# The second table's rows of the first token tile, gathered by token and summed on TensorE in 32-column strips

## The chip, the cores and the metric

The kernel runs on one core of a Trainium2 chip. The metric is the device time of one execution in microseconds (us); lower is better. PE is TensorE, PEld its weight loads, DVE VectorE, ACT ScalarE, POOL GpSimd, SP SyncE. A line of the kernel is written L842.

## The reference

One decoder layer on 512 tokens of 1024 channels: a token mixer (dilated and differential attention, gated, projected), then a retrieval over 16,384 single-neuron experts. The retrieval is what the change touches:

```python
q = (xt @ w_q).reshape(t, 8, 2, 128)               # 8 heads, two half queries
sc = einsum('thpd,pkd->thpk', q, sub_keys)         # 128 keys for each half
top_s, top_i = top_k(sc, 16)                       # 16 best of each half
...                                                # 16 best pairs of the 256: ids, gates
u = u_tab[ids]                                     # first table's rows (1024 channels)
act = gelu(einsum('cd,chkd->chk', x, u))
vv = v_tab[ids]                                    # second table's rows
out = einsum('chk,chkd->cd', gates * act, vv)      # 8 x 16 = 128 rows summed for each token
```

Then follow a second residual and a last norm. All of it is float32.

## The kernel before

The tokens are worked in two halves of two tiles of 128 tokens each. For each half, `mixer(b)` does both attentions, and `tail(b)` the gates, projections, second norm and the scores of the retrieval with their best keys. Weights come as units of 512 KB through a ring of seven places (`shared`, `wraw`); a unit is split into a high and a low part (ACT L290; DVE or POOL L291), and `mm3` (L379) multiplies in three products.

The retrieval is done in two ways. Tiles 2 and 3 (the second half) go through all experts: a table of gates is built (the loop with L1162 to L1175, here the table stage), and then 64 pairs of experts go through `s_part` (L379 into `s_ps`) and `v_part` (L1154 into `acc`): the expert stage. Tiles 0 and 1 (the first half) go by rows: `gather` (L812) is an indirect DMA that brings, for slot s, one row of a table for each of the 128 tokens of a tile, 128 x 1024 numbers, 512 KB, into a place of the same ring of seven. A slot is one of the 128 chosen pairs of a token. A row of the first table (u) is multiplied by the token's input and summed over the channels on DVE (L842). A row of the second table (v) is scaled by the slot's activation of each token and added to a sum on DVE (L852), or on PE (L871): for the first 56 slots of tile 0 (`NPE`), `by_rows_pe` (L863) has ACT write a diagonal matrix of the activations (L868), and PE multiplies it with the row into `pe_acc` (two matmuls of 512 columns).

The rows are side work for the second half of the tokens and for the expert stage. `by_rows` (L829) is a generator that issues one row at each step: 128 slots of u for tile 0, then 128 of u for tile 1, then 72 of v for tile 0, then 128 of v for tile 1. `pump(k)` (L323) lets it go on by `RATE[k]` rows (L38) at each weight unit, attention block, or slot of the table: "w" 2 for each weight unit of `mixer(1)`, "a" 0.75 for each attention block, "b" 2, "o1" 1.5 and "q1" 1.25 for each unit in `tail(1)`, "G" 0.45 for each of 64 steps of the table, "c" 0.76 for each of 256 units of the expert stage. `pump("")` issues what is left at the end. `pump_pe` (L875) does the same for the rows on PE, "pt" 2 for each of 16 heads in `choose_late`, and "pG" 0.4 for each step of the table. `ahead` (L818) gathers one row ahead (`LOOK`).

PSUM has eight banks. Until `tail(1)` comes to its scores the pool `ps` has three banks for products (`mm`), two for transposes (`tp`), two for scores and one for outputs; there `late_psum` (L1027) closes it and opens one with two banks for the row sums and one `tp`.

The instructions are put in order on each engine when the program is built; each engine then runs its own in that order.

Of the kernel before, what the change touches and what calls it, by code (L numbers as in the profile page):

```python
# [11 lines left out]
F32 = mybir.dt.float32  # L12
# [10 lines left out]
P = 128  # L23
# [25 lines left out]
NPE = 56  # L49
# [36 lines left out]
def block(ctx, tc, x, cT, w_ada, bT, b_row, g1T, norm2_g, w_in, w_pa, w_pb, w_out, lq1, lk1, lq2, lk2,  # L86
# [24 lines left out]
    def place_of(kind, nm, dt=F32):  # L111
        """a unit among the weights' places: raw, high and low parts; a third of the parts only in the front"""
# [8 lines left out]
    def front_place(i):  # L121
        """sixteen units of the front, none of which waits for another's place"""
# [24 lines left out]
    def rsqrt(v, n, nm):  # L147
        """1/sqrt(v), [P, n]"""
# [23 lines left out]
    # ---- small operands  # L172
# [18 lines left out]
    # ---- silu(c)  # L191
# [5 lines left out]
    # ---- modulation: sums over the eight rows of a partition, then over the partitions  # L197
# [24 lines left out]
    def first_modulation(i):  # L222
        """shift and scale of the channels 256 i .. 256 i + 256"""
# [22 lines left out]
    def mod_rows(sec, t):  # L246
        """sections 2..5 of the modulation, a row each in DRAM; the second scale with its norm's weights"""
# [25 lines left out]
    # ---- first norm  # L273
# [80 lines left out]
    def cols(src, kt, c0, nm):  # L354
        """128 columns, for use as the stationary side"""
# [11 lines left out]
    def cols256(src, kt, c0, nm):  # L367
        """256 columns, for use as the moving side"""
# [4 lines left out]
    def mm3(out_ps, a, b, kt, last=0):  # L373
        """sum over k of a.T @ b, both in two parts; last: the side whose low part is used last"""
# [10 lines left out]
    # ---- relative position bias, as bands  # L385
# [20 lines left out]
    def bias_band(t, h, at, o, m, w):  # L406
        """t[p, at + i w + j] = vec[head, o + i LEN_D + p + j], i < m: rows of a block in reverse"""
# [4 lines left out]
    # ---- lambda  # L412
# [16 lines left out]
    # queries by head: head s of a pair keeps its half of the rows, the other half is zero. The queries of a block  # L429
    # stand in reverse, as the bands do; the transpose of the outputs turns them back.  # L430
# [12 lines left out]
    # ---- keys and values of the first half wait in DRAM for the second  # L443
# [3 lines left out]
    def query(hin, c0, q, nm):  # L447
        """q: [P, 2, HW]"""
# [8 lines left out]
    def key(b, hin, c0, k, i):  # L457
        """k: [P, T]"""
# [24 lines left out]
    # ---- dilated attention: the three groups of a head share one softmax, which is what their merge by  # L483
    # denominators amounts to
# [87 lines left out]
    def diff_finish(ob, dst, h0):  # L572
        """norm of two heads' outputs, ob: [P, 2, HW], transposed and split into dst"""
# [21 lines left out]
    def mixer(b, between):  # L595
        """attention of half b: both branches' outputs in two parts, channels on partitions"""
# [49 lines left out]
    # ---- the retrieval's choice  # L646
# [8 lines left out]
    def begin_topk(n, t):  # L655
        """t: [P, 768]"""
# [14 lines left out]
    # a pair of ranks (i, j) can be among the best sixteen only if (i + 1)(j + 1) <= 16: row 0 whole, eight of  # L671
    # rows 1..7, one of rows 8..15, in the order of the full table
# [4 lines left out]
    def choose(n, h0, nh, out):  # L677
        """row and column keys of the chosen pairs, heads h0 .. h0 + nh: two [P, 16 nh], a slot a column"""
# [150 lines left out]
    def by_rows(ids, gates, h2_row, make):  # L829
# [5 lines left out]
        for v, n, s in order:  # L835
# [5 lines left out]
            if v == 0:  # L841
                nc.vector.scalar_tensor_tensor(r, r, 1.0, h2, op0=ALU.mult, op1=ALU.mult, accum_out=a)  # L842
                if s == P - 1:
                    nc.scalar.activation(act[n], act[n], AF.Gelu_apprx_tanh)
                    nc.vector.tensor_mul(act[n], act[n], gates[n])
                    if n == 0:
                        on_pe.append(by_rows_pe(ids[0]))
# [383 lines left out]
```

## Time and profile before

| | |
|---|---|
| time, median of three runs | 2154.51 us (2152.59 to 2160.33) |
| span of the profiled execution | 2148.4 us |
| busy, share of the span | PE 87%, DVE 86%, POOL 59%, ACT 45% |
| DMA | 588.00 MB, mean 274 GB/s; gathers 268.47 MB of it |
| mean granted TensorE clock | 0.952 of full speed |

The page gives no separate time for the profiled execution: its span is 6.1 us under the median of the runs, and that difference stands for what lies around the span. A span is from the first instruction to the last. Busy time of an engine is the time in which one of its instructions ran.

### The profile page before, as it was taken

How to read it: one execution, taken by the hardware profiler on the slowest of the kernel's cores; microseconds unless marked ns; L12 is line 12 of the kernel's file. 1: busy time of each engine (PE TensorE's matmuls, PEld its weight loads, DVE VectorE, ACT ScalarE, POOL GpSimd, SP SyncE). 2: the span in 40 equal slices, each digit the busy share in tenths (PEclk: the TensorE clock that was granted, in tenths of full speed). 3: DMA queues.
4: the chain of work that ended last, by engine and by line, in shares of the span. 5: the costliest groups of instructions: out<-in, count | busy, mean ns of one | idle time of the engine just before them, and what ended most of it. 6: DMA issues, size and time to landing. Idle time of an engine off the chain costs nothing.

```text
span 2148.4 us, 34562 instructions
## 1 busy us (share of the span) xinstructions
PE 1875.4 (87%) x12324; PEld 1668.1 (78%) x12324; DVE 1839.9 (86%) x3515; ACT 970.7 (45%) x1725; POOL 1257.4 (59%) x797
## 2 busy tenths in 40 slices
PE   6999989887778799878687877889999999999995
PEld 6889889887666687768684455678988889998885
DVE  7757865689999999899889999978999898888777
ACT  2544575442333356543232366534444444444442
POOL 2323323456676676667675766667675665655564
PEclk9999999999999999989798999999999999999998
DMA  9968766758898999889956755788888999998886
GB/s 296 281 198 255 212 178 178 233 175 265 281 313 280 315 325 315 295 291 307 304 186 228 251 169 184 247 284 309 316 316 313 343 346 324 342 335 309 306 308 236
DMA packets 369889, 588.00 MB, mean 274 GB/s; under 512 B 24962, under 2 KB 261002, under 8 KB 369716
## 3 DMA queue, kind: packets, MB, share of 16 engines
q1 hardware_dynamic: 295700, 316.79, 45.3%
q0 software_dynamic: 73728, 268.47, 35.6%
q8 instruction: 97, 1.59, 0.3%
q14 instruction: 76, 0.62, 0.1%
q10 hardware_dynamic: 288, 0.52, 0.1%
HBM read 575.13 MB, written 10.58 MB: 273 GB/s over the span
## 4 chain that ended last, share of the span: by engine, by line
PE 37%; DVE 35%; DMA 14%; issue 8%; POOL 3%; ACT 2%; SPq 1%; POOLq 0%; DVEq 0%; ACTq 0%
PE mm L379 12%; PE acc L1154 9%; PE s_ps L379 9%; DVE grow L842 8%; DMA grow<-in_v_tab_dram,ids 7%; DVE one L1168 3%; DVE wacc L210 2%; DMA wa<-in_w_ada_dram 2%; POOL grow L814 1%; DVE elo L291 1%; DMA grow<-in_u_tab_dram,ids 1%; PE s_ps L1172 1%; DVE rep L666 1%; PE sc L509 1%; DVE acc_rows L852 1%
## 5 line engine op out<-in xcount | busy, mean ns | idle before, releaser
L814 POOL DMA_INDIRECT grow<-in_v_tab_dram,ids x256 | 331.8, 1296 | 300.8 <-DVE ga L852 59.0
L814 POOL DMA_INDIRECT grow<-in_u_tab_dram,ids x256 | 329.6, 1287 | 221.7 <-DVE grow L842 69.8
L842 DVE SCALAR_TENSOR_TENSOR grow<-grow,h 128x1024 f32<-128x1024 f32 x256 | 350.7, 1378 | 6.9 <-DMA grow<-in_u_tab_dram,ids 5.4
L290 ACT CAST ehi<-eraw 128x1024 fp32r<-128x1024 f32 x145 | 152.6, 1053 | 228.7 <-PE acc L1154 75.7
L852 DVE SCALAR_TENSOR_TENSOR ga<-grow,act,ga 128x1024 f32<-128x1024 f32 x127 | 162.8, 1282 | 58.2 <-DMA grow<-in_v_tab_dram,ids 57.6
L290 ACT CAST more<-eraw 128x1024 fp32r<-128x1024 f32 x111 | 116.7, 1051 | 152.7 <-PE acc L1154 62.1
L379 PEld LDWEIGHTS s_ps<-h2T,more 128*128 128x128 f32 x1320 | 166.5, 191 | 4.9 <-ACT more L290 0.2
L1154 PE MATMUL acc<-more,w 128*128 128x512 f32 x672 | 163.4, 392 | 7.3 <-DVE w L291 6.4
L379 PE MATMUL s_ps<-h2T,more 128*128 128x256 f32 x1320 | 168.2, 283 | 0.0
L1154 PE MATMUL acc<-ehi,w 128*128 128x512 f32 x576 | 151.3, 399 | 17.4 <-DVE w L291 14.8
L852 DVE SCALAR_TENSOR_TENSOR acc_rows<-grow,act,acc_rows 128x1024 f32<-128x1024 f32 x71 | 124.4, 1751 | 38.7 <-DMA grow<-in_v_tab_dram,ids 38.2
L1154 PEld LDWEIGHTS acc<-more,w 128*128 128x128 f32 x672 | 127.1, 189 | 34.7 <-DVE w L291 6.8
L379 PE MATMUL s_ps<-h2T,ehi 128*128 128x256 f32 x1168 | 152.0, 283 | 0.0
L379 PEld LDWEIGHTS s_ps<-h2T,ehi 128*128 128x128 f32 x1168 | 145.8, 192 | 0.6
L291 DVE TENSOR_TENSOR elo<-eraw,ehi 128x1024 fp32r<-128x1024 f32 x95 | 136.0, 1432 | 9.4 <-ACT ehi L290 9.2
L1154 PEld LDWEIGHTS acc<-ehi,w 128*128 128x128 f32 x576 | 103.7, 190 | 42.6 <-DVE w L291 21.6
L291 POOL TENSOR_TENSOR elo<-eraw,ehi 128x1024 fp32r<-128x1024 f32 x50 | 123.0, 2459 | 12.6 <-ACT ehi L290 11.8
L1168 DVE TENSOR_SCALAR one<-iota,idT 128x128 f32<-128x128 f32 x256 | 116.5, 534 | 0.3 <-ACT idT L1118 0.3
L379 PE MATMUL mm<-wh_v,h 128*128 128x256 f32 x640 | 102.0, 311 | 15.5 <-ACT wh_v L290 13.1
L1172 PEld LDWEIGHTS s_ps<-one 128*128 128x128 f32 x512 | 69.2, 203 | 54.4 <-ACT G L1175 22.2
L291 DVE TENSOR_TENSOR more<-eraw,more 128x1024 fp32r<-128x1024 f32 x75 | 103.7, 1384 | 6.7 <-ACT more L290 6.5
L871 PE MATMUL ga<-grow,diag 128*128 128x512 f32 x224 | 108.1, 627 | 0.1
(304 smaller groups left out, 4682.5 us busy)
## 6 DMA issues: line engine op xcount, KB each, us to landing
eraw<-in_uT_dram SPq DMA_DIRECT2D x128, 512.0 KB
eraw<-in_v_tab_dram SPq DMA_DIRECT2D x128, 512.0 KB
wa<-in_w_ada_dram SPq DMA_DIRECT2D x48, 512.0 KB
w_v<-in_w_in_dram SPq DMA_DIRECT2D x40, 512.0 KB
w_k<-in_w_in_dram SPq DMA_DIRECT2D x40, 512.0 KB
w_gl<-in_w_in_dram SPq DMA_DIRECT2D x32, 512.0 KB
w_wql<-in_w_q_dram SPq DMA_DIRECT2D x32, 512.0 KB
w_q<-in_w_in_dram SPq DMA_DIRECT2D x24, 512.0 KB
```

The source lines that it names most:

```text
L210: nc.vector.scalar_tensor_tensor(acc, wa[:, k, :], c, acc, op0=ALU.mult, op1=ALU.add)
L290: nc.scalar.copy(hi, src)
L291: (eng or nc.vector).tensor_sub(lo, src, hi.bitcast(F32))
L379: r = nc.tensor.matmul(out_ps, a(i, k), b(j, k), start=(n == 0), stop=(n == 3 * kt - 1))
L509: nc.tensor.matmul(pS[:, at[g] - o:at[g] - o + w[g]], q[g][:, s, n * P:(n + 1) * P], k3[g][:, first[g] * P:(gn + 1) * P], start=True, stop ...
L814: nc.gpsimd.indirect_dma_start(out=r, out_offset=None, in_=tab, in_offset=bass.IndirectOffsetOnAxis(ap=ids[:, s:s + 1], axis=0))
L842: nc.vector.scalar_tensor_tensor(r, r, 1.0, h2, op0=ALU.mult, op1=ALU.mult, accum_out=a)
L852: nc.vector.scalar_tensor_tensor(acc[n], r, a, acc[n], op0=ALU.mult, op1=ALU.add)
L871: nc.tensor.matmul(pe_acc[0][:, sl], dg, r[:, sl], start=(s == 0), stop=(s == NPE - 1), skip_group_check=True)
L1154: nc.tensor.matmul(acc[b][hf], w[i][:, 256 * j + P * b:256 * j + P * b + P], V[jj][:, hf, :], start=(e == 0 and i + jj == 0), stop=(e == N ...
L1168: nc.vector.tensor_scalar(o1[:, t, :], iota, idT[:, 0, t0 + t:t0 + t + 1], idT[:, 2, t0 + t:t0 + t + 1], op0=ALU.is_equal, op1=ALU.mult)
L1172: last = nc.tensor.matmul(pg[:, t * P:(t + 1) * P], o2[:, t, :], o1[:, t, :], start=True, stop=True)
```

## The change

For tile 0 the second table is gathered by token: the 128 partitions of a gathered block are the 128 slots of one token. The chosen keys are transposed for that (`idsT`), and so are the activations. The weighted sum over the partitions is then a product with one column of weights for a token. `strips(g)` makes, for 32 tokens at a time, 32 strips of 128 x 32, all zero but for column i of strip i, which holds the activations of token i; `token_sum` multiplies the strip with the row's four quarters of 256 channels, each into another quarter of 32 PSUM partitions, so that 32 tokens gather in one 128 x 256 sum. `close_part` copies such a sum out (ACT) and sends it to DRAM by four DMAs; `last_norm(0)` reads it back.

The order of the steps becomes: u of tile 0 (128), v of tile 0 by token (128, on PE), u of tile 1 (128), v of tile 1 (128, on DVE). The diagonal way (`by_rows_pe`, `pump_pe`, `NPE`) goes. "pt" becomes 0.75 and drives the one generator in `choose_late`, "pG" goes, "c" becomes 0.92. A PSUM bank (`vp`) is opened for the token sums ahead of `mixer(1)`, which runs with two `mm` banks in place of three; `late_psum` goes. The zeroed strips lie in the place `h0`, which `G0` takes later.

```diff
-RATE = {"w": 2, "a": 0.75, "b": 2, "o1": 1.5, "q1": 1.25, "q0": 0, "r0": 0.5, "o0": 0, "pt": 2, "G": 0.45, "pG": 0.4,
-        "c": 0.76}
+RATE = {"w": 2, "a": 0.75, "b": 2, "o1": 1.5, "q1": 1.25, "q0": 0, "r0": 0.5, "o0": 0, "pt": 0.75, "G": 0.45,
+        "c": 0.92}
-NPE = 56
...
+    def open_strips():
+        z = wp.tile([P, 3, D], F32, name="strips", tag="h0")
+        nc.gpsimd.memset(z, 0.0)
+        parts["z"] = z
+
+    def strips(g):
+        if g < 3:
+            z = parts["z"][:, g, :]
+        else:
+            z = shared("strips3")
+            nc.gpsimd.memset(z, 0.0)
+        nc.scalar.copy(z[:, 0:D:33], act[0][:, 32 * g:32 * g + 32])
+        return z.rearrange("p (t c) -> p t c", t=32)
+
+    def close_part():
+        if "acc" not in parts:
+            return
+        acc, g, t0, t1 = parts.pop("acc"), *parts["at"]
+        st = shared("st")[:, 0:256]
+        nc.scalar.copy(st, acc)
+        for q in range(4):
+            nc.sync.dma_start(acc_dr[32 * g + t0:32 * g + t1, 256 * q:256 * q + 256], st[32 * q + t0:32 * q + t1, :])
+
+    def token_sum(t, r):
+        g, i = t // 32, t % 32
+        if i == 0:
+            parts["strips"] = strips(g)
+        first = "acc" not in parts
+        if first:
+            parts["acc"], parts["at"] = token_ps(), (g, i, 32)
+        acc, at = parts["acc"], parts["at"]
+        parts["at"] = (g, at[1], i + 1)
+        for q in range(4):
+            nc.tensor.matmul(acc[32 * q:32 * q + 32, :], parts["strips"][:, i, :], r[:, 256 * q:256 * q + 256],
+                             start=first, stop=True, skip_group_check=True)
+        if i == 31:
+            close_part()
...
+    def by_rows(h2_row, make):
+        order = [(u_tab, ids[0], s) for s in range(P)] + [(v_tab, idsT, t) for t in range(P)] + \
+                [(u_tab, ids[1], s) for s in range(P)] + [(v_tab, ids[1], s) for s in range(P)]
...
+            row_acts(n)
+            if n == 0:
+                pt = tp_ps()
+                nc.tensor.transpose(pt[:, 0:P], act[0], ident)
+                nc.scalar.copy(act[0], pt[:, 0:P])
+                for t in range(P):
+                    token_sum(t, next(rows))
+                    yield 2
...
         for h in range(nh):
             top16(cand[:, h, :], best[:, h, :], bj[:, h, :])
-            pump_pe("pt")
+            if n > 1:
+                pump("pt")
...
+        if n == 0 and h0 + nh == 8:
+            pt = tp_ps()
+            nc.tensor.transpose(pt[:, 0:P], idf, ident)
+            nc.vector.tensor_copy(idsT, pt[:, 0:P])
...
+    open_strips()
+    ps_guard.__exit__(None, None, None)
+    vp_guard = tc.tile_pool(name="vp", bufs=1, space=PSUM)
+    pools["vp"] = vp_guard.__enter__()
+    ps_guard = tc.tile_pool(name="ps1", bufs=1, space=PSUM)
+    pools.update(ps=ps_guard.__enter__(), mm=2)
...
+    while "strips" not in parts or parts["at"][0] < 2 or (parts["at"][0] == 2 and "acc" in parts):
+        next(running[0])
+    close_part()
+    G0 = wp.tile([P, 2 * EARLY, 256], F32, name="G0", tag="h0")
+    ps_guard.__exit__(None, None, None)
+    vp_guard.__exit__(None, None, None)
+    pools["ga"] = ctx.enter_context(tc.tile_pool(name="gp", bufs=1, space=PSUM))
```

## Rows read from the trace of the kernel before

**Rows 1.** Busy time of each engine by stretch; columns as in the first line

```profile
core 0: us, PE busy (x) PEld busy (x) DVE busy (x) ACT busy (x) POOL busy (x), PEclk, DMA share, GB/s
470.00:800.00 330.00, 263.42 (x1804) 235.24 (x1802) 319.26 (x846) 122.42 (x213) 224.80 (x146) 0.93 0.88 295
800.00:1150.00 350.00, 271.94 (x1884) 251.86 (x1884) 318.83 (x675) 154.01 (x320) 238.52 (x154) 0.88 0.84 276
1150.00:1372.00 222.00, 182.86 (x773) 116.25 (x774) 221.45 (x661) 113.66 (x289) 150.13 (x135) 0.93 0.65 212
1372.00:2134.00 762.00, 729.85 (x4614) 658.04 (x4612) 643.21 (x520) 337.11 (x390) 476.79 (x283) 0.99 0.88 317
```

**Rows 2.** The same stretches, u rows on DVE alone (L842, two records a row)

```profile
470.00:800.00 330.00, 160.50 (x231) 0.93 0.88 295
800.00:1150.00 350.00, 155.20 (x223) 0.88 0.84 276
1150.00:1372.00 222.00, 36.78 (x60) 0.93 0.65 212
```

**Rows 3.** The same, gathers issued on POOL (L814), last stretch

```profile
1372.00:2134.00 762.00, 264.05 (x197) 0.99 0.88 317
```

**Rows 4.** The same, three-product matmuls on PE alone (L379), second stretch

```profile
800.00:1150.00 350.00, 222.91 (x1564) 209.12 (x1564) 0.88 0.84 276
```

**Rows 5.** Chain that ended last, in order of time: start, us, what

```profile
349.04 72.54 PE mm L379 x612
...
1205.49 6.62 DMA grow<-in_v_tab_dram,ids
...
1376.82 14.41 DMA grow<-in_v_tab_dram,ids x3
...
1734.54 5.47 PE acc L1154 x24
1740.01 5.75 PE s_ps L379 x48
...
2118.48 9.74 DMA grow<-in_v_tab_dram,ids
```

**Rows 6.** Instructions in order of time, PE, around matmuls with one weight column

```profile
138.17 1.88 PE L255 MATMUL mm<-wacc,ones 128*1 128x512 f32 x4
139.98 0.66 PE L528 MATMUL tp<-ident,L 128*128 128x128 f32 x4
```

**Rows 7.** The same stretch, weight loads

```profile
138.17 0.09 PEld L255 LDWEIGHTS mm<-wacc,ones 128*1 128x1 f32 x2
138.60 0.08 PEld L255 LDWEIGHTS mm<-wacc,ones 128*1 128x1 f32 x1 [0.35 <-issue]
139.03 0.08 PEld L255 LDWEIGHTS mm<-wacc,ones 128*1 128x1 f32 x1 [0.35 <-issue]
139.98 0.42 PEld L528 LDWEIGHTS tp<-ident,L 128*128 128x128 f32 x4 [0.86 <-issue]
```

**Rows 8.** In order of time, PE: one row by a diagonal, sixteen table matmuls

```profile
1238.24 1.88 PE L871 MATMUL ga<-grow,diag 128*128 128x512 f32 x4
1239.95 2.35 PE L1172 MATMUL s_ps<-one 128*128 128x128 f32 x16
```

**Rows 9.** Costliest groups, DVE, 1372 to 2134: busy, mean ns, idle before

```profile
L852 DVE SCALAR_TENSOR_TENSOR ga<-grow,act,ga 128x1024 f32<-128x1024 f32 x127 | 162.8, 1282 | 58.2 <-DMA grow<-in_v_tab_dram,ids 57.6
...
L852 DVE SCALAR_TENSOR_TENSOR acc_rows<-grow,act,acc_rows 128x1024 f32<-128x1024 f32 x71 | 124.4, 1751 | 38.7 <-DMA grow<-in_v_tab_dram,ids 38.2
```

**Rows 10.** Stretches of the expert stage, ACT's gelu alone (L1107, one a pair)

```profile
1372.00:1722.00 350.00, 17.19 (x29) 1.00 0.87 312
1722.00:1970.00 248.00, 13.01 (x22) 1.00 0.92 333
```

**Rows 11.** What POOL waited for, 1372 to 2134: us, times, longest

```profile
POOL grow L814 <- DVE ga L852: 59.0, 28, 4.6
POOL grow L814 <- DVE elo L291: 49.4, 27, 4.2
POOL grow L814 <- DVE acc_rows L852: 35.4, 20, 4.5
POOL grow L814 <- DVE more L291: 35.1, 18, 4.4
```

**Rows 12.** One line's instructions (L842): ns min, median, max; first, last start

```profile
L842 DVE SCALAR_TENSOR_TENSOR grow<-grow,h x256: 1186/1212/4037, 477.6 to 1367.1; 128x1024 f32<-128x1024 f32 x128
```

More of the change, by code (lines that the diff above doesn't have):

```diff
@@ L861, in block @@
-    on_pe, pe_credit = [], {}
-    def by_rows_pe(ids):
-        rows = ahead([(v_tab, ids, s) for s in range(NPE)])
-        for s in range(NPE):
-            r = next(rows)
-            dg = next_diag()
-            nc.scalar.activation(dg, ident, AF.Copy, scale=act[0][:, s:s + 1])
-            for hf in range(2):
-                sl = slice(512 * hf, 512 * hf + 512)
-                nc.tensor.matmul(pe_acc[0][:, sl], dg, r[:, sl], start=(s == 0), stop=(s == NPE - 1),
-                                 skip_group_check=True)
-            yield
@@ L875, in pump_pe @@
-    def pump_pe(k):
-        if on_pe and pe_acc:
-            n = pe_credit.get(k, 0) + (RATE[k] if k else 1 << 20)
-            while n >= 1 and on_pe:
-                n -= 1
-                if next(on_pe[0], 0) == 0:
-                    on_pe.pop()
-            pe_credit[k] = n
-    diags = []
-    def next_diag():
-        if not diags:
-            t = shared("diag").rearrange("p (a b) -> p a b", a=8)
-            diags.extend(t[:, i] for i in range(8))
-        return diags.pop(0)
+    act, parts = {}, {}
@@ new lines, in block @@
+    acc_dr = dr.tile([P, D], F32, name="acc_dr")
+    def open_strips():
[18 more added lines that the diff above has]
+            nc.sync.dma_start(acc_dr[32 * g + t0:32 * g + t1, 256 * q:256 * q + 256], st[32 * q + t0:32 * q + t1, :])
@@ new lines, in row_acts @@
+    def row_acts(n):
+        nc.scalar.activation(act[n], act[n], AF.Gelu_apprx_tanh)
+        nc.vector.tensor_mul(act[n], act[n], gates[n])
+    def by_rows(h2_row, make):
+        order = [(u_tab, ids[0], s) for s in range(P)] + [(v_tab, idsT, t) for t in range(P)] + \
+                [(u_tab, ids[1], s) for s in range(P)] + [(v_tab, ids[1], s) for s in range(P)]
+        rows = ahead(order)
+        for n in range(2):
+            for s in range(P):
+                r = next(rows)
+                if s == 0:
+                    h2 = h2_row(n)
+                    act[n] = sb.tile([P, P], F32, name=f"act{n}", tag="gate0" if n else "act0")
+                nc.vector.scalar_tensor_tensor(r, r, 1.0, h2, op0=ALU.mult, op1=ALU.mult, accum_out=act[n][:, s:s + 1])
+                yield n
+            row_acts(n)
[6 more added lines that the diff above has]
+                    yield 2
+                parts["done"] = True
+        acc0 = grow()
+        nc.sync.dma_start(acc0, acc_dr)
+        last_norm(0, [acc0[:, 0:512], acc0[:, 512:1024]])
+        yield 3
+        acc = make()
+        for s in range(P):
+            r = next(rows)
+            a = act[1][:, s:s + 1]
+            if s == 0:
+                nc.vector.tensor_scalar(acc, r, a, None, op0=ALU.mult)
+            else:
+                nc.vector.scalar_tensor_tensor(acc, r, a, acc, op0=ALU.mult, op1=ALU.add)
+            yield 3
+        last_norm(1, [acc[:, 0:512], acc[:, 512:1024]])
+        yield 3
@@ L1020, in h2_row, with make_acc, token_ps @@
         return r
[L1022 to L1035 removed]
+    def make_acc():
+        return pools["ga"].tile([P, D], F32, name="ga2", tag="ga")
+    def token_ps():
+        if "ga" in pools:
+            return pools["ga"].tile([P, D], F32, name="vp2", tag="ga")[:, 0:256]
+        return pools["vp"].tile([P, 512], F32, name="vp", tag="vp")[:, 0:256]
+    idf = sb.tile([P, P], F32, name="idf")
+    idsT = idf.bitcast(I32)
     def retrieve(h):
@@ L1107, in activations @@
         nc.scalar.activation(dst, S, AF.Gelu_apprx_tanh)
-    G0 = wp.tile([P, 2 * EARLY, 256], F32, name="G0", tag="h0")
     low[:] = [nc.gpsimd]
```

52 lines of the change are left out of this document (4 added, 48 removed).

## The prediction

> **What bounds the kernel now.** I read the busy time by stretch first [rows 1]. Up to 470 us the change reaches nothing. From 470 to 1372 us the second half of the tokens is worked with rows beside it, and VectorE is the fullest engine: 319 of 330 us, 319 of 350, 221 of 222. A full engine runs at 0.97 of a stretch there, and I use that share below. PE has 272 of 350 us in the second stretch, at a granted clock of 0.88. DMA is close behind with 0.84 to 0.88 of its engines' time. In the expert stage, from 1372 us on, PE has 730 of 762 us.
>
> Then the u rows on DVE [rows 2]: 155 us of the second stretch are theirs (two records a row, so 111 rows). This is what the change can take away. Then the chain of waits [rows 5]: a pair of experts costs PE 5.47 + 5.75 = 11.22 us where nothing holds it. 64 pairs make 718 us, so the expert stage can't give much and has 44 us above that floor. Gathers stand on the chain where it begins and where it ends. Last, pairs by stretch [rows 10]: 29 pairs in the first 350 us are 12.07 us each, and 22 in the next 248 are 11.27.
>
> **Which rows move where.** The steps come out of RATE and the loops. Until the end of `tail(1)` 227 rows are issued, before and after: 3, then 60 units x 2 and 32 blocks x 0.75 in `mixer(1)`, then 24 x 2, 8 x 1.5 and 16 x 1.25. Before, 227 rows are 128 of tile 0's u and 99 of tile 1's. After, the 99 are token rows on PE. `choose_late` adds 16 x 0.75 = 12 token rows where 32 diagonal rows stood. The table adds 64 x 0.45 = 29: the last 17 token rows and 12 u rows, where it had 29 u rows and 24 on PE. The expert stage takes 256 x 0.92 = 235 and the end 11, which is 116 rows of u and 128 of v. Before it was 195 and 8; the trace has 197 gathers behind 1372 us [rows 3]. So DVE is freed ahead of 1372 us and pays behind it.
>
> **The price of a token row.** No row shows strips in different column groups. The nearest is a product with one weight column: four records of 512 columns take 1.88 us, their loads 0.43 us apart [rows 6, 7]. A token row streams just as much: four strips, two records each of 256 columns. One after the other that is 1.88 us, the upper bound, and as much as a diagonal row costs [rows 8]. If all of it ran at once in four groups it would be a quarter, 0.47 us, the lower bound. Between them: the two records of one strip follow each other on the same columns, as in [rows 7], and only the next strip's first can run beside the second. That leaves about four of eight steps, 0.94 us. I take this, since the records go in order. The change between narrow and wide is small: the last narrow load starts at 139.03, streams until about 139.89, and the first wide load starts at 139.98 [rows 7]. I add 0.1 us: 1.05 us a row, bounds 0.57 and 1.98.
>
> The nearest statement is in the Trainium skill, "TensorEngine Tiling (Array Packing)", Key Properties: column tiles work independently and in parallel, but a change of the tiling mode drains the engine. The drain agrees with the 0.1 us above. By the parallel part a row is the 0.57 us, which is the first rival; no row here shows it.
>
> **800 to 1150 us.** PE's own work: 1564 three-product matmuls [rows 4] at 72.54/612 = 0.1185 us, the pace of a stretch where PE waits for nothing [rows 5], are 185 us. The rest of PE is 272 - 223 = 49 us. With 99 rows at 1.05 us that is 234 + 104 = 338 us, and at 0.97 of the stretch 348. DVE falls from 319 us to about 319 - 99 x 1.4 = 180 and is out of the way. DMA's 0.84 x 350 = 294 us is unchanged. So PE takes the place of DVE as the bound, and the stretch goes from 350 to 348 us: -2. Behind a token row in PE's order stand all the products of `tail(1)`. A gather that lands late now stops them, where it stopped only DVE before. Gathers have stood long on the chain [rows 5], but in this stretch a lagging PE covers them.
>
> **470 to 800 us.** These rows are u of tile 0 in both kernels. `mm` has two banks in place of three. The cover is that DVE is the bound there and PE idles a fifth of the stretch [rows 1]. I allow +2 us, between 0 and 12. The zeroing of the strips on POOL (225 of 330 us busy), two transposes and five `close_part` with four DMAs each go behind POOL's and PE's slack at nothing. Without that cover they would cost a few us.
>
> **1150 to 1372 us.** DVE bounds it. 30 u rows cost 36.8 us there [rows 2], 1.23 each; 12 remain: 18 x 1.23 = -22 us. PE loses 108 us of diagonals ([rows 8], 56 of them at 1.93) and takes 29 x 1.05 = 30. Before, PE's order had diagonal rows ahead of the transposes of the keys, with one gather of 6.62 us on the chain [rows 5]. I count half of it, -3 us. DVE stays the bound: 221 - 22 of about 197.
>
> **Expert stage.** 44 more rows in the ring, u rows in its first part. DVE: 116 x 1.75 + 128 x 1.28 = 367 us against 163 + 124 = 287 [rows 9], so 643 + 80 = 723 us. I take 1.75 for a u row since it reads SBUF alone as `acc_rows` does; at its 1.19 minimum [rows 12] 65 us less. 723 us is 95% of 762, under the 97% that DVE can reach: the lower bound is 0. The upper bound is the ring of seven. A pair takes 4 + 3.68 places in place of 4 + 3.04, 1.09 times as many, and POOL already waits for places that DVE frees [rows 11]. If every place is held as long as now, the first 31.5 pairs go from 12.07 to 13.17 us, +35 us. The others, with DMA at 0.92 x 1.09 = 1.0 [rows 10], add up to +10. I take +18 of 0 to 45, nearer the low end, since DVE and PE both still fit. At the end three more rows of 1.28 us wait before the last norms: +4, since the last gather ends the chain [rows 5].
>
> **Sum:** -2 + 2 - 22 - 3 + 18 + 4 = -3 us. On the span of 2148.4 us that is 2145.4, and with the 6.1 us that the median lies above it, 2151.5 us. The change lifts DVE's load and puts as much on PE.
>
> **Rivals.**
> 1. Four groups at once: 0.57 us a row. PE has 234 + 56 = 290 us, DMA 294, so the stretch from 800 us is 294/0.97 = 303: -47 in place of -2. Time 2106 us. For it: the strips lie in separate columns. Against it: two records of a strip share theirs.
> 2. The strips run one after another: 1.98 us a row. 234 + 196 = 430, at 0.97 443 us: +93 in place of -2. Time 2246 us. For it: the only narrow matmuls seen are 0.43 us apart; they are in one group, so they say nothing against overlap. It ends on the slower side from about 1.2 us a row on: each 0.1 us above 1.05 adds 10 us.
> 3. The ring decides: gathers for 244 rows hold the places of the experts' units. Then the expert stage costs +45 in place of +18, time 2178 us. For it: POOL's waits [rows 11] and the gathers on the chain. Against it: in the second part PE is at 248 of 248 us though the ring is full.
>
> **How the numbers follow.** Half a per cent, 11 us, is about what a measurement of this kernel tells from no change. The forecast has 0.48, rival 1 0.18, rival 2 0.27, rival 3 0.07. The forecast's own range is 2125 to 2180 us, from the bounds of the expert stage and 0.2 us a row either way. Of its 0.48, 0.21 is faster by over 0.5%, 0.16 within and 0.11 slower. With the rivals: faster 0.21 + 0.18 = 0.39, within 0.16 + 0.02 = 0.18 (a mild rival 3), slower 0.11 + 0.27 + 0.05 = 0.43. The range goes from 2095 us (rival 1 with a cheap expert stage) to 2240 us, which leaves out about half of rival 2 and little below: 0.18 in all.
>
> **What would show it.** The matmuls of the strips: starts of a row's eight records within about 1 us are the forecast, 0.5 the first rival, 1.8 the second. From 800 to 1150 us PE should be at 0.95 or more, with a granted clock near 1.0, and DVE near 0.5; PE waiting for gathers there would prove my cover wrong. The table stage should be some 20 us shorter. The expert stage should have DVE at 0.92 or more and pairs of 12 to 12.5 us in its first half. If it stays at 762 us, or goes beyond 800, my price of the moved rows is wrong.

## The result and the profile after

The changed kernel takes 2221.07 us (median of four runs, 2217.12 to 2223.02) against 2155.12 us (2152.59 to 2160.33) of the kernel before, measured beside it. The ratio is 1.0304 [1.027, 1.0337]: slower. The span of the profiled execution is 2215.0 us, 66.6 us above the 2148.4 of before. The time lies inside the range I gave, but my forecast was no change, and I put the upper end of the range there for strips that run one after another (my second rival), which they do not; that it held is luck. Over the span PE is busy for 85% and DVE for 79% (87 and 86 before), at a mean granted clock of 0.927 (0.952); the bytes are nearly the same, 589.14 MB against 588.00.

Busy time by stretch, the same stretches as in [rows 1], with one more for the longer end:

```profile
core 0: us, PE busy (x) PEld busy (x) DVE busy (x) ACT busy (x) POOL busy (x), PEclk, DMA share, GB/s
470.00:800.00 330.00, 248.01 (x1688) 223.89 (x1687) 293.70 (x812) 113.35 (x193) 210.58 (x135) 0.86 0.84 274
800.00:1150.00 350.00, 310.82 (x2479) 246.44 (x2482) 179.17 (x404) 152.41 (x321) 199.45 (x149) 0.94 0.82 273
1150.00:1372.00 222.00, 140.74 (x1039) 108.36 (x1030) 199.90 (x700) 97.84 (x236) 126.86 (x106) 0.78 0.47 150
1372.00:2134.00 762.00, 710.75 (x4409) 633.67 (x4410) 674.49 (x661) 327.98 (x391) 496.54 (x304) 0.98 0.90 320
2134.00:2215.00 81.00, 44.15 (x257) 37.72 (x255) 65.34 (x88) 23.75 (x33) 38.73 (x28) 0.81 0.76 271
```

The u rows alone, where [rows 2] had 155 and 37 us in the second and third stretch (L888 here):

```profile
800.00:1150.00 350.00, 32.76 (x42) 0.94 0.82 273
1150.00:1372.00 222.00, 16.17 (x27) 0.78 0.47 150
1372.00:2134.00 762.00, 159.14 (x230) 0.98 0.90 320
```

DVE is indeed freed in the second stretch, 179 us in place of 319, and pays in the fourth, 674 in place of 643. DMA's share falls in the third, 0.47 in place of 0.65, and rises in the fourth. But the stages move against these fixed stretches, so I compare by events. Each number below is the start of an instruction on PE in the trace of that kernel (the last score product is the last one with the query weights of the retrieval, in `tail(1)`); the last column is the end of the span. A line with a plus adds to "after, keys later".

```
kernel                      mixer(1)  last     first    first    last     end
                            first     score    table    expert   expert
                            product   product  matmul   v_part   v_part
before                       493.1    1153.9   1218.8   1384.9   2133.5   2148.4
after                        542.8    1187.6   1251.3   1402.0   2180.7   2215.0
before, two banks            495.3    1188.1   1252.9   1418.3   2169.7   2183.9
before, two banks + keys     543.2    1187.1   1251.8   1417.9   2165.3   2179.7
before, three banks anew     497.3    1148.8   1213.7   1379.8   2134.2   2148.9
after, keys later            494.0    1176.0   1239.4   1390.6   2168.6   2201.6
 + third bank                497.4    1176.8   1241.7   1390.7   2162.3   2195.7
 + u rows between            497.1    1166.7   1228.3   1361.9   2133.4   2165.5
   and no token gathers      495.2    1143.9   1205.5   1332.1   2105.5   2137.4
after, 44 u rows fewer       548.0    1192.0   1255.5   1402.5   2144.3   2160.1
after, one column group      545.4    1273.2   1338.7   1489.4   2271.9   2306.4
rows placed anew             498.2    1176.1   1245.3   1390.7   2115.0   2136.2
 three mm banks, one tp      501.2    1183.3   1248.4   1391.2   2115.4   2135.0
 three mm banks, shared      497.5    1159.4   1227.5   1369.7   2100.1   2119.3
```

The first two lines give the whole loss: +49.7 us at the start of `mixer(1)`, +33.7 at the last score product, +32.5 at the table, +17.1 at the first `v_part`, +47.2 at the last, +66.6 at the end. So the table stage gained 15 us (153.5 to 138.1 us from its first matmul to its last), the expert stage lost 30 (748.6 to 778.7), and the end behind the last product lost 19 (14.9 to 34.3).

The start first. Instructions of PE in order of time, at the change from the first half of the tokens to the second:

```profile
492.72 0.94 PE L740 MATMUL sc<-sk_sb,qtl 128*128 128x128 f32 x6 [0.30 <-ACT qtl L1027]
536.66 0.48 PE L1078 MATMUL tp<-ident,idf 128*128 128x128 f32 x1 [43.00 <-DVE idf L1071]
542.82 0.55 PE L378 MATMUL mm<-wh_v,h 128*128 128x256 f32 x1 [5.69 <-DVE idf L1079]
```

One transposition of 0.48 us, that of the chosen keys, stands in PE's order ahead of every product of `mixer(1)`, and it waits 43.00 us for DVE's choice of the keys. The new PSUM pool is opened behind it. DVE's own work goes on meanwhile, 47.12 of 50 us:

```profile
500.00:550.00 50.00, 7.66 (x51) 7.39 (x52) 47.12 (x204) 2.44 (x4) 14.60 (x13) 0.54 0.74 226
```

The price of a token row, in the same view:

```profile
1005.82 0.64 PE L868 MATMUL vp<-grow,strips 128*32 128x256 f32 x8
1006.38 2.17 PE L378 MATMUL mm<-ob,wh_pl 128*128 128x256 f32 x16
```

All eight records of a row start and hand over to the next product within 0.56 us. That is the lower bound of my range, not the 1.05 us that I took. By the starts in this trace, rows that stand back to back follow each other in 0.43 us, and a row between full products takes 0.57 (the median of 67), so the change of form takes about 0.14 us.

Where tile 0's u rows end and its token rows begin, first POOL, then DVE and PE in order of time, then the busy time from 850 to 900 us:

```profile
870.62 0.95 POOL L814 DMA_INDIRECT grow<-in_v_tab_dram,idf  x1 [6.30 <-DVE dst L555]
894.00 0.94 POOL L814 DMA_INDIRECT grow<-in_v_tab_dram,idf  x1 [22.43 <-PE vp L868]
```

```profile
856.15 0.29 DVE L875 TENSOR_TENSOR act<-act,gate 128x128 f32<-128x128 f32 x1 [1.48 <-ACT act L874]
```

```profile
891.04 0.27 PE L893 MATMUL tp<-ident,act 128*128 128x128 f32 x1
892.63 2.58 PE L868 MATMUL vp<-grow,strips 128*32 128x256 f32 x44
```

```profile
850.00:900.00 50.00, 43.06 (x303) 33.99 (x304) 29.14 (x88) 36.62 (x91) 14.73 (x14) 0.93 0.48 163
```

The activations of tile 0 are ready on DVE at 856.4 us (L875), but their transposition comes to its turn on PE at 891.04. Token rows gathered ahead sit in the places of the ring meanwhile, so POOL waits 22.43 us for a place and the DMA share falls to 0.48. I call this the ring lock.

In the expert stage, the costliest groups of DVE from 1389 to 2181 us (columns as in [rows 9]), then the pairs (ACT's gelu, L1135 here, as in [rows 10]) by stretch, counted from the end of the table stage on, and one record of that line:

```profile
L910 DVE SCALAR_TENSOR_TENSOR ga<-grow,act,ga 128x1024 f32<-128x1024 f32 x121 | 155.0, 1281 | 13.8 <-DMA grow<-in_v_tab_dram,ids 13.0
L888 DVE SCALAR_TENSOR_TENSOR grow<-grow,h 128x1024 f32<-128x1024 f32 x111 | 154.3, 1397 | 24.3 <-DMA grow<-in_u_tab_dram,ids 24.1
```

```profile
1389.00:1739.00 350.00, 18.61 (x30) 0.99 0.90 317
1739.00:1987.00 248.00, 11.95 (x20) 0.98 0.93 333
```

```profile
1396.77 1.28 ACT L1135 ACT_TABLE_LOAD   x1
```

One of the 30 records is the load of a table of ACT and no pair, so the first 350 us hold 29 pairs, as before. Whole pairs in a stretch are a coarse count; the starts of each pair's first `v_part` product tell more:

```
kernel                     pair 1   pair 33  pair 64   us a pair, 1 to 33   33 to 64
before                     1384.9   1768.0   2120.0    11.97                11.35
after                      1402.0   1800.1   2174.4    12.44                12.07
after, 44 u rows fewer     1402.5   1785.0   2131.5    11.95                11.18
```

Both halves are slower, the first by 15 us and the second by 22; the last pair gives 7 back (6.3 us against 13.5). DMA moves 333 GB/s in that second part in both kernels, so it is the same transfer rate that carries fewer pairs. And the end, DVE in order of time, with the gather that stands last on the chain:

```profile
2194.66 1.29 DVE L910 SCALAR_TENSOR_TENSOR ga<-grow,act,ga 128x1024 f32<-128x1024 f32 x1 [1.19 <-DMA grow<-in_v_tab_dram,ids]
```

```profile
2183.76 10.80 DMA grow<-in_v_tab_dram,ids
```

The last row is added 14 us behind the last product; before, the last gather was issued ahead of it [rows 5].

### The profile page after: what moved, and what is told of

Its sections match the earlier page's. It is cut to its first block, busy times and chain, and to the rows that moved or that the text cites. A ratio compares the mean times of both kernels' runs of the same rounds, so it can differ in the third digit from the quotient of the medians.

```text
span 2215.0 us, 36094 instructions
## 1 busy us (share of the span) xinstructions
PE 1878.2 (85%) x13126; PEld 1653.0 (75%) x13126; DVE 1743.5 (79%) x3443; ACT 955.4 (43%) x1679; POOL 1233.4 (56%) x799
## 2 busy tenths in 40 slices
DMA packets 370806, 589.14 MB, mean 266 GB/s; under 512 B 25234, under 2 KB 261786, under 8 KB 370628
## 3 DMA queue, kind: packets, MB, share of 16 engines
q0 software_dynamic: 73728, 268.47, 34.8%
## 5 line engine op out<-in xcount | busy, mean ns | idle before, releaser
L814 POOL DMA_INDIRECT grow<-in_u_tab_dram,ids x256 | 357.4, 1396 | 244.9 <-DVE grow L888 74.2
L888 DVE SCALAR_TENSOR_TENSOR grow<-grow,h 128x1024 f32<-128x1024 f32 x256 | 350.1, 1377 | 44.7 <-DMA grow<-in_u_tab_dram,ids 43.5
L814 POOL DMA_INDIRECT grow<-in_v_tab_dram,ids x128 | 151.3, 1182 | 146.0 <-DVE ga L910 57.6
L814 POOL DMA_INDIRECT grow<-in_v_tab_dram,idf x128 | 127.6, 997 | 132.6 <-PE vp L868 78.0
L378 PE MATMUL s_ps<-h2T,more 128*128 128x256 f32 x1320 | 173.0, 284 | 10.1 <-POOL more L290 9.7
L290 DVE TENSOR_TENSOR more<-eraw,more 128x1024 fp32r<-128x1024 f32 x75 | 122.8, 1637 | 25.6 <-ACT more L289 25.1
L1205 PE MATMUL s_ps<-one 128*128 128x128 f32 x512 | 92.7, 339 | 36.7 <-DVE one L1201 20.5
L1205 PEld LDWEIGHTS s_ps<-one 128*128 128x128 f32 x512 | 80.8, 237 | 53.2 <-ACT one L1199 19.6
```

What stands on the lines that cost most here:

```text
L290: (eng or nc.vector).tensor_sub(lo, src, hi.bitcast(F32))
L378: r = nc.tensor.matmul(out_ps, a(i, k), b(j, k), start=(n == 0), stop=(n == 3 * kt - 1))
L814: nc.gpsimd.indirect_dma_start(out=r, out_offset=None, in_=tab, in_offset=bass.IndirectOffsetOnAxis(ap=ids[:, s:s + 1], axis=0))
L1205: last = nc.tensor.matmul(pg[:, t * P:(t + 1) * P], o2[:, t, :], o1[:, t, :], start=True, stop=True)
```

## The experiments

Medians of before beside these runs lie between 2147.31 and 2148.26 us; each ratio is to those.

**The four column groups made one.** All strips go to the first 32 partitions, so the four quarters of the channels of tile 0 are added into one.

```diff
-            nc.tensor.matmul(acc[32 * q:32 * q + 32, :], parts["strips"][:, i, :], ...
+            nc.tensor.matmul(acc[0:32, :], parts["strips"][:, i, :], ...
```

> The four strips of a token row all go into the first 32 PSUM partitions, so that the four quarters of the channels of tile 0's sum are added together and the output of tile 0 is not the reference's. The work streamed is the same. Theory (four column groups run at once): a token row takes about 1.8 us in place of 0.57; PE gets 1.25 x 111 = 140 us more between 890 and 1210 us, where it is nearly full, and the kernel is 80 to 140 us longer: 2300 to 2360 us. Rival (narrow products are cheap by themselves, in any columns): a row stays near 0.6 us and the time within 10 us of the changed kernel.

2303.74 us, 1.0709 [1.0648, 1.0771]. PE in order of time:

```profile
1004.10 1.91 PE L868 MATMUL vp<-grow,strips 128*32 128x256 f32 x8
1005.94 2.15 PE L378 MATMUL mm<-ob,wh_pl 128*128 128x256 f32 x16
```

The same eight records now take 1.84 us. So the 0.56 us is the overlap of the four groups: the mechanism of my first rival, with its price. All strips write the same PSUM partitions here too, so the run does not tell the columns of the array from the places in PSUM.

**The keys transposed later.** The transposition and its copy stand behind the opening of the new pool.

```diff
-        if n == 0 and h0 + nh == 8:
-            pt = tp_ps()
-            nc.tensor.transpose(pt[:, 0:P], idf, ident)
-            nc.vector.tensor_copy(idsT, pt[:, 0:P])
...
     pools.update(ps=ps_guard.__enter__(), mm=2)
+    pt = tp_ps()
+    nc.tensor.transpose(pt[:, 0:P], idf, ident)
+    nc.vector.tensor_copy(idsT, pt[:, 0:P])
```

> The transposition of tile 0's keys stands behind the change of the PSUM pools, among the first products of the second mixer; all else is the changed kernel. Theory (TensorE's order is blocked): PE no longer waits 43 us for the last four heads' keys, the first product of the second mixer starts at about 495 us in place of 543, and since VectorE becomes full again until the token rows begin, 30 to 45 us of the 50 come back: 2175 to 2190 us. Rival (the wait is covered, since VectorE works on rows meanwhile and has the less to do later): the first product starts as early, but the time stays within 10 us of the changed kernel, 2211 to 2231.

2203.57 us, 1.024 [1.0178, 1.0302]. The second mixer starts at 494.0, 49 us sooner, yet the last score product comes only 12 us and the end 13 us sooner. The time lies between what I expected and what the rival gave; both missed. While PE stands still in the changed kernel DVE works on, and what it did then it need not do later, so most of the 43 us were no loss. Part of the rest goes at the ring lock: tile 0's u rows end 14 us sooner (840.1 against 854.3), its first token row comes 10 us sooner (882.8 against 892.6).

**The kernel before with that block, and with two banks alone.** The first has the last 64 keys transposed in the old pool, then the pool closed, a bank held and `mm` at two; the second has only the pool and the two banks; the third has the pool closed and opened anew with three banks.

```diff
+    ps_guard.__exit__(None, None, None)
+    vp_guard = tc.tile_pool(name="vp", bufs=1, space=PSUM)
+    vp_guard.__enter__().tile([P, 512], F32, name="vp", tag="vp")
+    ps_guard = tc.tile_pool(name="ps1", bufs=1, space=PSUM)
+    pools.update(ps=ps_guard.__enter__(), mm=2)
     oa, ob, finish = mixer(1, relieve)
```

> The kernel before, with only this added: the last 64 keys of tile 0 are transposed on PE into the old PSUM pool and copied, nobody reads them; then the pool is closed, one bank is held unused, and the second mixer runs with two banks for products. Theory (the block costs by itself): PE is idle for some 45 us from about 495 us on and the kernel takes 2185 to 2205 us. Rival (the loss belongs to the new order of the rows): within 10 us of the kernel before, 2145 to 2165.

> The kernel before, with the PSUM pool closed and opened anew ahead of the second mixer, one bank held unused and two banks for products there; no keys are transposed. Theory (the place of the transposition in TensorE's order is what blocks, not the pool): the second mixer starts at about 495 us and the time is within 10 us of the kernel before. Rival (closing the pool, or the third bank, costs): 15 to 35 us more than before.

> The kernel before, with the pool closed and opened anew ahead of the second mixer as in the run with two banks, but with three banks for products again and none held; nothing of the rows is changed. The run with two banks took 35 us more of span than the kernel before (2183.9 against 2148.4), though its second mixer starts within 2 us of before. Theory: the third bank is what costs; with two, the products of one block can't be placed ahead of the scores of the one before, and the order on PE is another. Then this run is within 12 us of before, 2140 to 2160 us. Rival: closing the pool costs, since every bank of the new one waits for the last use of the old; then it keeps the 35 us, 2175 to 2195 us.

With the block 2178.34 us, 1.0123 [1.0064, 1.0183]; with two banks alone 2189.07 us, 1.0202 [1.0151, 1.0252]; with three banks 2149.19 us, 0.9996 [0.9973, 1.002]. The first lies between the theory and the rival, though PE stood as expected (its second mixer starts at 543.2). My theory for the second run fell: two banks cost the kernel before 35.5 us of span (41 by the medians), the keys' block nothing on top (2179.7 against 2183.9), and closing the pool nothing (2148.9). PE in order of time, with two banks and then before:

```profile
639.23 1.67 PE L379 MATMUL mm<-wl_v,h 128*128 128x256 f32 x12
652.45 2.50 PE L509 MATMUL sc<-k,qz 128*128 128x384 f32 x4 [11.54 <-DVE st L517]
```

```profile
640.29 2.05 PE L379 MATMUL mm<-h,wh_q 128*128 128x256 f32 x16
643.23 1.20 PE L379 MATMUL mm<-h,wl_q 128*128 128x256 f32 x8 [0.90 <-POOL wl_q L291]
645.28 2.18 PE L379 MATMUL mm<-h,wh_k 128*128 128x256 f32 x16 [0.86 <-ACT qz L454]
647.30 1.12 PE L379 MATMUL mm<-h,wl_k 128*128 128x256 f32 x8
649.83 1.34 PE L509 MATMUL sc<-k,qz 128*128 128x384 f32 x4 [1.41 <-DVE st L517]
```

Both have finished the values of a pair of heads at 640 us. Before, a whole query and key product stand ahead of the scores that wait for DVE; with two banks PE's order has the scores next, and PE stands for 11.54 us. The order is written when the program is built, so a bank less changes the order, not only a wait in it. The Trainium skill ("Perfetto Trace Analysis", Optimizing Tensor Performance, Matmuls) asks that independent products rotate through different PSUM banks so that one's evacuation overlaps the next; these three runs agree that the third bank is worth 35.5 us, here through the order.

**44 u rows fewer.** Of tile 1's u rows the last 44 are left out, their activations set to zero, and "c" is 0.76 again.

```diff
-        "c": 0.92}
+        "c": 0.76}
...
-                [(u_tab, ids[1], s) for s in range(P)] + ...
+                [(u_tab, ids[1], s) for s in range(84)] + ...
```

> Left out: 44 of tile 1's 128 rows of the first table, their activations set to zero; with 0.76 rows a unit the expert stage has 195 rows as in the kernel before. Theory (the rows moved into the expert stage cost 30 us there and part of the 19 us at the end): expert products span about 750 us in place of 779, and the kernel takes 2175 to 2190 us. Rival (the expert stage is longer for its u rows on VectorE, or for where it starts, and not for how many rows): over 2205 us.

2160.39 us, 1.0041 [1.0011, 1.007]: 61 us less than the changed kernel, and below the 2175 to 2190 us that I expected. The stages before the experts do not move (first `v_part` at 1402.5 against 1402.0); the expert stage takes 741.8 us and the end 15.8. From 1752 to 2000 us, this run and then the changed kernel:

```profile
1752.00:2000.00 248.00, 248.00 (x1590) 226.63 (x1590) 221.22 (x172) 116.28 (x134) 159.62 (x99) 1.00 0.93 335
```

```profile
1752.00:2000.00 248.00, 232.19 (x1431) 206.52 (x1430) 220.90 (x191) 105.40 (x123) 155.01 (x99) 0.98 0.93 334
```

The transfers are equal, 335 and 334 GB/s; PE is full with fewer rows and has 16 us of gaps with more. DVE has 221 us in both. The same rate does not make it the ceiling of the transfers: in the kernel before PE is full at 333 GB/s too, and 356 GB/s were moved over 50 us.

```profile
1722.00:1970.00 248.00, 247.56 (x1590) 226.08 (x1590) 215.43 (x172) 115.01 (x132) 151.41 (x98) 1.00 0.92 333
1700.00:1750.00 50.00, 49.23 (x306) 44.12 (x306) 47.00 (x36) 24.75 (x28) 33.36 (x21) 1.00 0.96 356
```

SyncE's queue, which loads the experts' units, waits for some 206 of these 248 us with 44 rows fewer and for 208 in the changed kernel, nearly all for places of the ring. So the rows themselves cost, and DVE's load is not why; whether they cost through the ring's places, as my third rival had it, or through the transfers, no run separates.

**U rows between.** On top of the later keys, 16 of tile 1's u rows are done between tile 0's u rows and its token rows. Then the same without the gathers of the token rows: the strips are multiplied with their own tile, so that the sum of tile 0 is left out in substance, and PE's work stays.

```diff
+        seq = [("u0", s) for s in range(P)] + [("u1", s) for s in range(16)]
+        seq += [("t", t) for t in range(P)] + [("u1", s) for s in range(16, P)]
```

> As the run with the keys transposed later, and 16 u rows of tile 1 stand between tile 0's u rows and its token rows; the rows a unit are as in the changed kernel. Theory (token rows gathered ahead of their activations fill all seven places of the ring, and POOL's next gather and the weights wait about 21 us): that one wait goes, and the run is 10 to 25 us under the run with the keys transposed later, 2180 to 2195 us. Rival (the wait is covered by products that PE still has to do): no more than 5 us under it, 2198 us and over.

> As the run with u rows between, but the 128 gathers of token rows are left out: the strips are multiplied with their own tile, so tile 0's output is not the reference's; PE's matmuls are as many and as large. Theory (from 880 to 1180 us DMA and the ring of places are the bound, with PE close behind, so that freeing VectorE gave nothing): that stretch, from the first token row to the last score product, is 30 to 60 us shorter than in the run with u rows between, with PE over 0.95. Rival (PE is the bound there): no more than 10 us shorter.

2174.87 us, 1.0144 [1.0084, 1.0204], 29 us under the run with the later keys and so more than I expected, and without the gathers 2135.8 us, 0.9948 [0.9923, 0.9974]. From 830 to 880 us, with 16 rows between, then with only the keys mended, with what POOL waited for there from 820 to 900 (us, times, longest):

```profile
830.00:880.00 50.00, 43.59 (x297) 38.10 (x296) 43.45 (x90) 31.51 (x74) 36.00 (x24) 0.97 0.81 269
```

```profile
830.00:880.00 50.00, 44.34 (x275) 36.01 (x274) 33.91 (x91) 34.57 (x86) 19.60 (x13) 0.93 0.48 161
```

```profile
POOL grow L814 <- PE vp L868: 24.4, 2, 21.4
```

The ring lock is gone. Of the 36 us of span between these two runs, 11 come ahead of the table. The table stage gives 20 (138.4 to 118.4 us): its 29 steps of rows held 12 u rows and now hold none, which is 12 x 1.23 = 15 us of DVE by the price of [rows 2]. The rest is in the expert stage and at the end. The gathers of the token rows cost 23 us ahead of the last score product; from the first token row to it the stretch is 27 us shorter without them, a little under the 30 to 60 that I expected. From 900 to 1150 us, with the gathers and without:

```profile
900.00:1150.00 250.00, 233.43 (x2042) 190.00 (x2041) 114.74 (x327) 101.29 (x198) 153.07 (x112) 0.97 0.84 275
```

```profile
900.00:1150.00 250.00, 248.98 (x2302) 208.54 (x2304) 131.63 (x428) 109.23 (x215) 85.03 (x39) 1.00 0.41 116
```

Without them PE is full, 249 of 250 us, at a granted clock of 1.00 (2.4 GHz). With them it stands for 17 us. DVE is at about half in both. PE does not stand for the token rows themselves: in the run with gathers none of its waits in this stretch is for one, and in the changed kernel one is. That one wait, then the longest one of the queue that loads the weights (SyncE) in the changed kernel, then the same queue's longest before, all from 900 to 1150 us (us, times, longest):

```profile
PE vp L868 <- DMA grow<-in_v_tab_dram,idf: 1.0, 1, 1.0
```

```profile
SPq L341 <- PE vp L868: 111.0, 25, 9.3
```

```profile
SPq L342 <- DVE grow L842: 77.7, 17, 8.5
```

A token row keeps its place of the ring until PE comes to it, and the next weights wait for the place. Without the gathers that wait is gone, and so is most of the traffic (116 GB/s against 275); which of the two gives the 23 us was not tested.

**Rows placed anew.** The later keys; eight u rows of tile 1 between, then 60 token rows alternating with 43 u rows; more rows into `tail(1)` and the table, fewer into the expert stage.

```diff
-"q1": 1.25, ... "pt": 0.75, "G": 0.45, "c": 0.92
+"q1": 2, ... "pt": 2.25, "G": 0.5, "c": 0.78
...
+        seq = [("u0", s) for s in range(P)] + [("u1", s) for s in range(8)]
+        for i in range(60):
+            seq += [("t", i)] + [("u1", 8 + s) for s in range(43 * i // 60, 43 * (i + 1) // 60)]
+        seq += [("t", t) for t in range(60, P)] + [("u1", s) for s in range(51, P)]
```

> As the run with the keys transposed later, with the side rows placed anew: after tile 0's u rows 8 u rows of tile 1, then 60 token rows and 43 u rows in turn, then the other token rows (36 in the late choice of keys, 32 with the table, where VectorE is full), then the rest; 2 rows a unit in the score stage, 0.78 a unit with the experts, which leaves 7 for the end. Theory (the changed kernel lost by the block, by 44 rows moved to the experts and by the late end, and the strips themselves are cheap): the block, the 30 us and the 19 us go while the table stays 15 to 30 us shorter, 2115 to 2145 us, under the kernel before. Rival (token rows cost more than they free, wherever they stand): 2150 us and over.

2128.65 us, 0.9911 [0.9885, 0.9938]: faster than both kernels. Gathers from 1380 us on are 200, against 239 in the changed kernel and 195 before (POOL's busy time and count, after and then before):

```profile
1380.00:2220.00 840.00, 314.11 (x239) 0.97 0.89 315
1380.00:2220.00 840.00, 259.48 (x195) 0.99 0.80 286
```

The expert stage takes 724.3 us and PE is full in its second part:

```profile
1741.00:1989.00 248.00, 247.55 (x1587) 225.55 (x1586) 227.38 (x172) 114.58 (x132) 153.97 (x99) 1.00 0.92 332
```

Ahead of the table this kernel is still 26.5 us behind before; all that it gains, it gains behind it.

**The third bank given back.** Three banks for products and one for transposes; then three, two and two, with the token sums in the half of the attentions' output bank that is not used; then this last in the changed kernel's own order of rows, with the later keys. In the two runs with the shared bank the output is no longer the reference's: they price the bank and are no kernels to use. The Trainium skill ("PSUM — Partial Sum Buffer", The four PSUM rules) has it that two sums open in one bank and the same partitions can't both begin with a clearing product; no run here tests that.

```diff
-    pools.update(ps=ps_guard.__enter__(), mm=2)
+    pools.update(ps=ps_guard.__enter__(), mm=3, tp=1)
```

> The run with the rows placed anew (2128.65 us), with three banks for products and one for transposes in place of two and two from the second mixer on. Theory: the third bank for products gives back most of what two cost the kernel before, 20 to 35 us, and one bank for transposes costs less: 2095 to 2115 us. Rival: one bank for transposes takes as much (they stand between a block's scores and its values), or closing the pool is what costs: 2125 to 2145 us.

> The run with the rows placed anew, with three banks for products, two for transposes and two for scores: the token sums lie in the half of the attentions' output bank that is not used. Theory: the bank is what the second mixer and its tail lacked (three banks in the kernel before without any other change: no loss; two: 35 us; one for transposes in place of two: no gain over two for products), so 20 to 35 us come back of 2128.65: 2095 to 2110 us. Rival: with the order of the rows as it stands, the stretch from 900 us on is bound by PE and the transfers in any case, and what the mixer regains is lost there; then 2118 to 2132 us.

> The changed kernel with the keys transposed behind the new pool (2203.57 us) and with the token sums in the free half of the output bank, so that three banks for products stay; the order of the rows and their rates are those of the change. Theory: the two blocks (keys and bank) are most of what the change lost ahead of the table, so the bank gives 20 to 35 us here too: 2168 to 2184 us, and what is left above before is the rows' order and the expert stage. Rival: the row order with its ring locked in 830 to 880 us takes up what the bank gives: 2190 to 2205 us.

2132.63 us, 0.9922 [0.9897, 0.9946]; 2120.12 us, 0.9864 [0.9817, 0.991]; 2203.28 us, 1.0263 [1.0211, 1.0315]. A bank taken from the transposes costs about what a bank taken from the products costs. In the new order of rows the third bank gives 8.5 us by the medians and 17 by the spans, where 20 to 35 were expected; all three times lie where the rival put them. The mixer does regain what the bank cost: its last product with `wh_v` starts at 852.0 us with the shared bank, at 884.5 with two banks and at 849.9 before; about half of that is lost by the last score product. In the change's own order it gives nothing that can be told (2203.57 to 2203.28 us): the u rows end sooner, but the ring locks sooner too. What POOL waited for in that run, 820 to 900 us (us, times, longest), and its busy time from 830 to 880:

```profile
POOL grow L817 <- PE vp L871: 27.2, 4, 20.8
```

```profile
830.00:880.00 50.00, 36.50 (x221) 26.66 (x220) 22.07 (x79) 33.79 (x89) 10.51 (x8) 0.91 0.38 129
```

## Why the prediction was wrong

The direction failed, not the list of parts. By its own steps:

- **Which rows move where** was right. 239 gathers behind 1380 us against 195 are the 44 more rows that I worked out.
- **The price of a token row** was mis-sized: 1.05 us taken, 0.56 measured. My argument was that the two records of a strip share its columns and so follow each other; the overlap hides that. The Trainium skill's statement that column tiles work in parallel ("TensorEngine Tiling (Array Packing)", Key Properties) agrees with the 0.56 against 1.84 us. This error leaned the other way: it made the forecast slower.
- **800 to 1150 us** gave -2 by that price, and -47 by the first rival's. Neither came. PE did take DVE's place as the fullest engine (311 of 350 us, 56 of them strips, against DVE's 179), but it is not full. I had feared gathers that land late and covered them with a lagging PE. That cover held: PE waited 1.0 us for them from 900 to 1150 (in the run with the rows placed anew it did wait, 27.8 us in all). What I put at nothing, with DMA's 294 us unchanged, is that a lagging PE keeps the ring's places, and the weights wait for those; how much of the 23 us is that, and how much the traffic, stays open. The ring lock adds 22 us in which hardly a row is brought, and I had not thought of it.
- **470 to 800 us: two banks in place of three, +2 of 0 to 12** was mis-sized. It is 35.5 us on the kernel before, for the order of PE's instructions, not for a wait on a bank: I counted on PE's idle fifth as cover, while the bank is what lets PE use that fifth. In the changed kernel the cost is hidden: there the lock and the gathers hold the same stretch, and the third bank returns 0 to 6 us.
- **The transpositions at nothing behind PE's slack.** The keys' one holds PE for 43 us. DVE works on meanwhile, so it costs 13 us of span in the changed kernel and nothing in the one before beside two banks. Not nothing, but not its length either.
- **1150 to 1372 us: -22 and -3** had the right sign and two thirds of its size: the table stage is 15 us shorter, with DVE at 200 of 222 us.
- **Expert stage +18, end +4** was the larger mistake in one term: +30 and +19, and 55 of span come back when the 44 rows and their rate are taken out. I sized it by DVE (0.95 of the stage; it is 0.885, as a u row took 1.40 us and not 1.75) and allowed the transfers up to 10 us. DVE had room, and the rows cost all the same, 55/44 = 1.25 us a row of span. A row is 0.524 MB (268.47 MB for 512 of them), at 333 GB/s 1.57 us, so 44 rows make 69 us of transfers; they also hold the ring's places. The third rival, the ring, had a size for it, +45, and is not excluded.

- **What would show it.** DVE at half from 800 us on came true (0.51), and so did pairs of 12 to 12.5 us in the first half of the experts (12.44). PE at 0.95 did not (0.89, at a granted clock of 0.94), nor did DVE at 0.92 in the expert stage.

So the sum that I made, -25 ahead of the experts and +22 behind, came out as +17 and +49. The steps that failed are these: ahead of the experts, the keys' transposition at nothing and the seam from u rows to token rows, which had no term; behind, the price of 44 moved rows. For the first two, the runs with the keys later and then with 16 u rows between bring the first table matmul from 1251.3 to 1239.4 and to 1228.3 us, which is 23 of the 32.5 us that it came late; how the other 9.5 divide between the bank and the gathers stays open. For the third, the run with 44 rows fewer gives 55 us back. The prices of the bank, the keys, the lock and the gathers (35, 13, 11 and 23 us) were taken in different kernels and do not add. Why a bank less makes just this order is not settled: I saw the order, not the reasons of what writes it.

## What to carry to other kernels

Work that is moved is not free of the stage it goes to: price it there by its transfers and its places in the ring too, not only by the engines' time (a gathered row cost 1.25 to 1.4 us in the expert stage, though DVE had room). Before taking a buffer from an engine that idles, ask whether its order would still let it run ahead; and when work that consumes a shared ring goes to an in-order engine, put other rows between its first and what it waits for. Here the same change with its keys transposed later, its rows placed so, and only five more of them than before in the last stage, went from 3% slower to 0.9% faster.

## What was not expected of the hardware

Two matmuls that follow each other on one 32-column strip still overlap with those of the other three: eight records of 379 ns each took 0.56 us in four column groups and 1.84 us in one, a factor of 3.3. And the transfers of the expert stage stayed at 332 to 335 GB/s in the second part, a DMA share of 0.92 to 0.93, in four kernels with 195 to 239 gathers in that stage; in three of the four PE is full there, so this is no measured ceiling.
